# Gated linear attention on one core: decays, keys and states one head at a time, output gates between the values, a norm's factors spread ahead of the heads

## The chip, the core and the metric

The kernel runs on one core of one Trainium2 chip. TensorE (PE) multiplies, VectorE (DVE) and ScalarE (ACT) do element-wise work, GpSimd (POOL) a few powers, SyncE (SP) issues the loads. The metric is the device time of one execution in microseconds (us); of the kernel before, the median of three executions is 2082.17 us (2081.37 to 2084.97).

## What is computed

The program computes two transformer blocks of two layers each on 256 tokens of width 1024. The change lies in the last layer's mixer, gated linear attention with 4 heads, key width 128 and value width 256 per head, run over 256 context tokens and 256 latent tokens in both directions, in chunks of 64:

```python
q = z[..., :512] * 128 ** -0.5; k = z[..., 512:1024]; v = z[..., 1024:2048]; out_gate = z[..., 2048:]
g_d = log_sigmoid((h @ w_gate_down[d]) @ w_gate_up[d] + gate_bias[d]) / 16      # d: two directions
b = cumsum(g, within a chunk)
A = where(lower, (q * exp(b)) @ (k * exp(-b)).T, 0)
o = A @ v + (q * exp(b)) @ S
S = exp(b_last) * S + (k * exp(b_last - b)).T @ v                               # the state, chunk by chunk
o = rms_norm(o_forward + o_backward, g_norm) * silu(out_gate)
x = x + m[2] * rms_norm(o @ w_o, g_post_mix)                                    # then the channel MLP
```

## The kernel before, in words

Every weight is a granule of 128 x 1024 floats (512 KB). `gran` (line 483) takes the next granule in the order that `plan()` (line 34) writes out: `ahead` (line 460) keeps loads (SP), the high part `wh` (ScalarE, line 471) and the low part `wl` (VectorE, line 477) a few granules ahead, then the granule's matmuls are issued as three products each (high by high, high by low, low by high). What has to happen with a result (a copy out of PSUM) is deferred to the next granule or to `flush`.

Work off the weights is written as generators, added with `add` (line 508). `tick` (line 515) advances every generator that is alive by one step, in the order in which they were added; each granule ends with one such round, and the `steps(2)` of the mixer issue two more. The program is issued in exactly this order (a manual schedule), and each engine runs its own instructions in the order of issue. So an instruction that waits holds up everything issued after it on its engine.

In `layer2_gla` (line 1910), the order before is: queries of four heads (`gq`), two gate granules of head 0 (`gg` 0 and 1), the projection for the decays (`gdown`), then `decay()` is added; keys of four heads (`gk`); then the values of heads 0 to 3, two granules each (`gv`, 48 matmuls of 128 x 256 a granule); gates 2 to 7, 24 matmuls a granule; then the output projection (`gwo`).

- `decay()` (line 1956) makes the two directions' decays. Its first rounds fall among the keys: two matmuls a head into PSUM, Abs and Exp on ScalarE. Then, in one round for all heads, Ln (line 1975, with a load of its table); in the next two rounds the subtractions (line 1979, 128 x 1024, one a head), two heads a round; in two more the scans (lines 1985 and 1986, 128 x 512, two a head). Only after that `ldone` lets the heads begin.
- `direction(hd, d)` (line 2004) issues, a round each: (1) two small VectorE operations that begin `ke`; (2) five Exps on ScalarE; (3) three products on VectorE, `ke` first; (4) four transposes of `ke` and two score matmuls on TensorE; (5) the copy `gkn` on ScalarE (line 2039); (6) the first state's matmuls, which need `v`; (7) to (10) three more state matmuls, each with a state update on VectorE (line 2055).
- `outputs(hd)` (line 2061) follows when both directions are done: the mask on VectorE (line 2065), the output matmuls, copies and squares, the norm, transposes, the multiplication with the gate `og` (line 2097) and the split into `goT`, which `gwo` reads.
- `head(hd, delay)` (line 2108) adds the two directions, the second two rounds later, and the outputs. Head 0 is added ahead of the values of head 1, head 1 ahead of the values of head 3, heads 2 and 3 after all values, with delays 1, 1, 0 and 5.
- `bcast_cols(gmix, "G")` (line 1399) spreads the factors of the norm after the mixer over the partitions: eight transposes into two banks, each copied out by ScalarE. Before, it stands after the values (line 2151).

Of the kernel before, what the change touches and what calls it, by code (L numbers as in the profile page):

```python
# [33 lines left out]
def plan():  # L34

    g = []

    def ws(key, w, l, c0):
        g.append((key, w, l, "ws", 0, c0))

    def nat(key, w, l, r0, c0):
        g.append((key, w, l, "nat", r0, c0))

    def qkv(st, cb):
        for kp in range(4):
            nat(("qkv", st, cb, kp), "attn_w_qkv_2", 0, kp * 256, cb * 512)

    def awo(st):
        for hf in range(2):
            for kp in range(4):  # L50
                nat(("awo", st, hf, kp), "attn_w_o_2", 0, kp * 256, hf * 512)

    def mi(q, st):
        for i in range(8):
            ws(("mi", 0, q * 8 + i, st), "w_mlp_in_2", 0, (q * 8 + i) * 128)

    def mo(q, st):
        for hf in range(2):
            for kp in range(4):
                nat(("mo", 0, q, hf, kp, st), "w_mlp_out_2", 0, q * 1024 + kp * 256, hf * 512)  # L60


    for l in range(2):
        if l == 0:
            for kp in range(4):
                for p in range(3):
                    nat(("va", l, p, kp), "w_in", l, kp * 256, a_col(2, p, 0))
                nat(("vm", l, 0, kp), "w_in", l, kp * 256, C_V)
        else:
            for n in range(12):  # L70
                nat(("va", l, n // 4, n % 4), "w_in", l, n % 4 * 256, a_col(2, n // 4, 0))
        g.append((("gates", l), "w_in", l, "gates", 0, C_G))
        for qd in range(2):
            for which in range(2):
                for p in range(3):
                    for j in range(2):
                        ws(("at", l, qd, which, p, j), "w_in", l, a_col(which, p, qd * 4 + j * 2))
        for h in range(1 - l, 2):
            for kp in range(4):
                nat(("vm", l, h, kp), "w_in", l, kp * 256, C_V + h * 512)  # L80
        for h in range(4):
            for which in range(2):
                for d in range(2):
                    ws(("qk", l, h, which, d), "w_in", l, C_QK + which * 1024 + h * 256 + d * 128)
            for j in range(2 * h, 2 * h + 2):
                ws(("o", l, j), "w_in", l, C_O + j * 128)
            for kind, j in EXTRA[h]:
                if kind == "br":
                    ws(("br", l, j), "w_in", l, C_BR + j * 128)
                else:  # L90
                    g.append((("wb", l, j), "w_b", l, "wsb", 0, j * 256))
        for j in range(8):
            ws(("wa", l, j), "w_a", l, j * 128)
        for j in range(8):
            ws(("wo", l, j), "w_out", l, j * 128)
        if l == 0:
            for cb in (2, 0, 1):
                qkv(1, cb)
        else:
            mi(0, 1)  # L100
        for n, i in FF:
            if n == 1:
                ws(("w1", l, i), "w1", l, i * 128)
                ws(("w3", l, i), "w3", l, i * 128)
            else:
                g.append((("w2", l, i), "w2", l, "row", i * 128, 0))
        if l == 0:
            awo(1)
        else:
            mo(0, 1)  # L110
            mi(1, 1)
    for cb in (2, 0, 1):
        qkv(0, cb)
    mo(1, 1)
    awo(0)
    mi(2, 1)
    for q in range(3):
        mi(q, 0)
        mo(q, 0 if q < 2 else 2)
    mi(3, 2)  # L120
    for st in range(2):
        mo(3, st)
    for h in range(4):
        ws(("gq", h), "gla_w_in_2", 0, h * 128)
    for j in range(2):
        ws(("gg", j), "gla_w_in_2", 0, 2048 + j * 128)
    g.append((("gdown",), "gla_w_gate_down_2", 0, "gdown", 0, 0))
    for h in range(4):
        ws(("gk", h), "gla_w_in_2", 0, 512 + h * 128)
    for h in range(4):  # L130
        for hf in range(2):
            g.append((("gv", h, hf), "gla_w_in_2", 0, "wsb", hf * 512, 1024 + h * 256))
    for j in range(2, 8):
        ws(("gg", j), "gla_w_in_2", 0, 2048 + j * 128)
    for hf in range(2):
        for kp in range(4):
            nat(("gwo", hf, kp), "gla_w_o_2", 0, kp * 256, hf * 512)
    for n, i in LAST:
        if n == "mi":
            ws(("mi", 1, i), "w_mlp_in_2", 1, i * 128)  # L140
        else:
            g.append((("mo", 1, i), "w_mlp_out_2", 1, "row", i * 128, 0))
    n = len(g)
    for w in ("w_ada", "w_mod_2"):
        for l in range(2):
            for v in ADA_ORDER:
                for j in range(8):
                    g.append(((w, l, v, j), w, l, "colT", 0, v * 1024 + j * 128))
    return g, n
# [192 lines left out]
class Core:  # L342
# [28 lines left out]
    @property  # L371
    def late(self):

        return self.dve - self.pe


class Kernel:
# [1532 lines left out]
    def layer2_gla(self, x, xc):  # L1910
        nc = self.nc
        h = self.h1
# [3 lines left out]
        for hd in range(4):  # L1916
            ps = self.mmb()
            self.grans2(("gq", hd), self.mm_ws(ps[:, 0:256], hl),
                        lambda hd=hd, ps=ps: nc.scalar.activation(out=qT[:, hd], in_=ps[:, 0:256], func=AF.Copy, scale=128 ** -0.5))
        bank = [None]  # L1920

        def gates(j0, j1, gran):

            for j in range(j0, j1):
                if j % 2 == 0:
                    bank[0] = self.mmb()
                ps = bank[0]

                def post(j=j, ps=ps):
                    th = self.t2("gth", (128, 2, 256))  # L1930
                    nc.scalar.activation(out=th, in_=self.pair(ps), func=AF.Tanh, scale=0.5)
                    nc.vector.scalar_tensor_tensor(out=og.pair[j // 2], in0=th, scalar=1.0, in1=self.pair(ps), op0=ALU.add, op1=ALU.mult)
                gran(("gg", j), self.mm_ws(ps[:, (j % 2) * 256:(j % 2) * 256 + 256], hl), post if j % 2 else None)
        gates(0, 2, self.grans2)
        h[1] = self.wait(h[1])
# [15 lines left out]
        lg, ee, ldone = [None] * 4, [None] * 4, []  # L1951
# [4 lines left out]
        def decay():  # L1956
# [17 lines left out]
            for hd in range(4):  # L1974
                nc.scalar.activation(out=ee[hd], in_=ee[hd], func=AF.Ln, bias=1.0)
            yield
            for hd in range(4):
                f = lg[hd].rearrange("p a b -> p (a b)")
                nc.vector.tensor_tensor(out=f, in0=f, in1=ee[hd].rearrange("p a b -> p (a b)"), op=ALU.subtract)
                if hd % 2:  # L1980
                    yield

            for hd in range(4):
                B = ee[hd]
                nc.vector.tensor_tensor_scan(out=B[:, 0], data0=reset[:, 0], data1=lg[hd][:, 0], initial=0.0, op0=ALU.mult, op1=ALU.add)
                nc.vector.tensor_tensor_scan(out=B[:, 1, ::-1], data0=reset[:, 1, ::-1], data1=lg[hd][:, 1, ::-1], initial=0.0,
                                             op0=ALU.mult, op1=ALU.add)
                if hd % 2:
                    yield
            ldone.append(1)  # L1990
        self.add(decay())
        kT = [self.tv("gkT", (128, 2, 512)) for _ in range(2)]
        for hd in range(4):
            ps = self.mmb()
            self.gran(("gk", hd), self.mm_ws2(ps, h), lambda hd=hd, ps=ps: nc.scalar.activation(out=kT[hd // 2][:, hd % 2], in_=ps, func=AF.Copy))
            if hd:
                self.tick(False)
        v = [None] * 4
        ss = self.small([128, 2, 4], "gss", 1)
        i16 = 1.0 / 16  # L2000
        order = (0, 1, 2, 3), (3, 2, 1, 0)
        H = [dict(S=[None, None], qd=[None, None], at=None, done=0) for _ in range(4)]

        def direction(hd, d):
            k = kT[hd // 2][:, hd % 2]
            B = ee[hd][:, d]
            last, tot = (B[:, 63:256:64], B[:, 511:512]) if d == 0 else (B[:, 0:256:64], B[:, 256:257])
# [30 lines left out]
            kn = H[hd]["kn"][:, d]  # L2038
            nc.scalar.activation(out=kn.rearrange("p a b -> p (a b)"), in_=tr, func=AF.Copy)
            yield  # L2040
            st = self.aux()
            for b in range(2):
                nc.tensor.matmul(st[:, 0:256], kn[:, 2 + b], v[hd][:, 2 + b], start=b == 0, stop=b == 1)
# [17 lines left out]
        def outputs(hd):  # L2061
# [28 lines left out]
            for jj in range(2):  # L2090
                for b in range(2):
                    nc.tensor.transpose(tr[:, jj * 256 + b * 128:jj * 256 + b * 128 + 128], on[:, b, jj * 128:(jj + 1) * 128], self.ident)
            yield
            o32 = self.t2("go32", (128, 2, 256))
            for jj in range(2):
                nc.scalar.activation(out=o32[:, jj], in_=tr[:, jj * 256:(jj + 1) * 256], func=AF.Copy, scale=gn[:, jj:jj + 1])
# [8 lines left out]
        ot = [None] * 4  # L2105
# [7 lines left out]
        def values(hd):  # L2113
# [18 lines left out]
                return f  # L2132
            for hf in range(2):
                self.gran(("gv", hd, hf), mm(hf))
                steps(2)
        while self.adaq:
            self.ada_step()
        gmix = self.gain_cols(1, "g_post_mix_2", 2, 0)
        cols = self.scales(1, "g_pre_mlp_2", 3, 4, (0,))
        for hd in range(4):  # L2140
            if hd == 1:
                self.until(lambda: ldone)
                head(0, 1)
            if hd == 3:
                head(1, 1)
            values(hd)
        self.flush()
        head(2, 0)
        head(3, 5)
        oT = Lazy(lambda k: ot[k // 2][:, k % 2])  # L2150
        G = self.bcast_cols(gmix, "G")
        for j in range(2, 8):
            gates(j, j + 1, self.gran)
            steps(2)
        self.flush()
        y = [[None] * 2 for _ in range(2)]
        for hf, bank in enumerate((self.mmb, self.aux)):
# [98 lines left out]
```

## Time and profile before

| what | us |
|---|---|
| median of three executions | 2082.17 |
| lowest and highest | 2081.37, 2084.97 |
| the profiled execution's own time | 2092.44 |
| its span, first to last instruction | 2090.7 |
| mean granted clock of TensorE | 0.993 |

The profile is of one execution; its times run from the start of its span. A group is a kind of instruction on one engine, named by what it writes and reads (`trb<-ident,ke` are transposes of `ke` into a PSUM bank of that name). An arrow behind an idle time names the instruction whose end let the engine go on.

### The profile page before, as it was taken

The page shows a single profiled execution, that of the slowest core. Times are in us where ns is not written, and L with a number is a line of the kernel's source. Part 1 is how long each engine was busy: PE and PEld are TensorE (multiplying, and loading weights), DVE is VectorE, ACT ScalarE, POOL GpSimd, SP SyncE. Part 2 cuts the span into 40 slices and gives each one's busy share as a digit, 9 for nine tenths or more (in the row PEclk, how much of TensorE's full clock was granted, in tenths as well). Part 3 has the DMA queues.
Part 4 walks back from the last instruction along what each step waited for, and adds up shares of the span by engine and source line. Part 5 has one row for each costly group of instructions (what it writes and reads, how often), then busy time and mean ns, then how long its engine had stood idle before and what let it go on. Part 6 is the DMA issues. An engine that isn't in the chain of part 4 may idle for free.

```text
span 2090.7 us, 38245 instructions
## 1 busy us (share of the span) xinstructions
PE 2030.9 (97%) x15176; PEld 1888.9 (90%) x15176; DVE 1586.6 (76%) x2717; ACT 1149.3 (55%) x1968; POOL 45.1 (2%) x63
## 2 busy tenths in 40 slices
PE   7999999999999999998999999999999999999998
PEld 6999998899998989998999988899998989877997
DVE  7788988799978989988899776777563485466555
ACT  5756665655546656665744455556542464445444
POOL 0000000000000000000000000000000010000000
PEclk9999999999999999999999999999999999999999
DMA  9786566598876886555589755115553352214553
GB/s 340 281 320 213 192 235 221 187 315 305 304 254 228 284 274 233 187 202 186 167 290 358 274 196 176 61 56 176 191 183 101 115 181 75 77 65 155 188 191 132
DMA packets 120884, 426.88 MB, mean 204 GB/s; under 512 B 13664, under 2 KB 18528, under 8 KB 120704
## 3 DMA queue, kind: packets, MB, share of 16 engines
q1 hardware_dynamic: 120704, 424.43, 59.1%
q8 instruction: 119, 1.95, 0.4%
q14 instruction: 61, 0.50, 0.1%
HBM read 423.33 MB, written 1.05 MB: 203 GB/s over the span
## 4 chain that ended last, share of the span: by engine, by line
PE 87%; DVE 7%; ACT 4%; issue 1%; DMA 1%; POOL 0%; DVEq 0%; POOLq 0%; SPq 0%; ACTq 0%
PE mm L338 54%; PE aux L338 28%; PE trb L338 5%; DVE wl L338 1%; ACT wh L471 1%; DVE yg L338 1%; POOL rs L674 0%; ACT xh L1467 0%; DVE mtmp L338 0%; DMA raw<-in_w 0%; DVE xh L338 0%; DVE x L338 0%; DVE araw L338 0%; ACT ah L912 0%; DVE ee L338 0%
## 5 line engine op out<-in xcount | busy, mean ns | idle before, releaser
L338 DVE TENSOR_TENSOR wl<-raw,wh 128x1024 fp32r<-128x1024 f32 x591 | 718.7, 1221 | 153.1 <-PE aux L338 71.5
L471 ACT ACTIVATE wh<-raw 128x1024 fp32r<-128x1024 f32 x591 | 623.6, 1059 | 336.2 <-PE mm L338 117.7
L338 PE MATMUL mm<-uT,wh 128*128 128x256 f32 x3488 | 622.3, 282 | 0.0
L338 PEld LDWEIGHTS mm<-uT,wh 128*128 128x128 f32 x3488 | 531.7, 188 | 2.2 <-ACT va L814 0.3
L338 PE MATMUL mm<-uT,wl 128*128 128x256 f32 x1744 | 487.0, 279 | 0.0
L338 PE MATMUL mm<-hT,wh 128*128 128x256 f32 x1888 | 339.4, 283 | 4.8 <-ACT y L1772 2.1
L338 PEld LDWEIGHTS mm<-uT,wl 128*128 128x128 f32 x1744 | 329.6, 189 | 0.0
L338 PEld LDWEIGHTS mm<-hT,wh 128*128 128x128 f32 x1888 | 292.7, 190 | 11.5 <-ACT y L1772 2.3
L338 PE MATMUL mm<-hT,wl 128*128 128x256 f32 x944 | 265.8, 282 | 0.0
L338 DVE CUSTOM_DVE_ANT_0 araw<-araw,silu 128x1024 f32<-128x1024 f32 x192 | 233.2, 1220 | 8.4 <-DMA araw<-in_w 5.9
L338 PE MATMUL aux<-wh,hid 128*128 128x512 f32 x640 | 199.9, 394 | 0.0
L338 PEld LDWEIGHTS mm<-hT,wl 128*128 128x128 f32 x944 | 181.4, 192 | 0.0
L338 PEld LDWEIGHTS aux<-wh,hid 128*128 128x128 f32 x640 | 117.7, 188 | 23.6 <-DVE hid L338 0.2
L338 DVE TENSOR_TENSOR r<-r 128x256 f32<-128x256 f32 (+1 forms) x88 | 39.5, 448 | 117.4 <-ACT r L1905 117.3
L338 PE MATMUL aux<-mlg,wh 128*128 128x256 f32 x704 | 127.1, 283 | 0.0
L338 PE MATMUL aux<-wl,hid 128*128 128x512 f32 x320 | 124.8, 390 | 0.0
L338 PEld LDWEIGHTS aux<-mlg,wh 128*128 128x128 f32 x704 | 107.3, 188 | 0.0
L1905 ACT ACTIVATE r<-mm 128x256 f32<-128x256 f32 (+1 forms) x88 | 35.7, 406 | 125.1 <-PE mm L338 125.1
L338 PE MATMUL aux<-mlg,wl 128*128 128x256 f32 x352 | 98.8, 281 | 0.0
L674 POOL TENSOR_TENSOR rs<-ve,mhalf 128x1 f32<-128x1 f32 (+1 forms) x48 | 41.8, 871 | 2040.5 <-DVE ve L338 1853.0
L338 DVE CUSTOM_DVE_ANT_0 junk<-araw,silu 128x1024 bf16<-128x1024 f32 x64 | 77.9, 1218 | 0.0
L338 PE MATMUL mm<-wh,hT 128*128 128x256 f32 (+1 forms) x352 | 76.8, 316 | 0.6 <-DVE qs L338 0.6
(365 smaller groups left out, 3081.7 us busy)
## 6 DMA issues: line engine op xcount, KB each, us to landing
raw<-in_w SPq DMA_DIRECT2D x591, 512.0 KB, 3.9
araw<-in_w SPq DMA_DIRECT2D x192, 512.0 KB, 5.2
abias<-in_abias SPq DMA_DIRECT2D x32, 192.0 KB, 5.6
xc<-in_ctx SPq DMA_DIRECT2D x4, 512.0 KB, 6.1
x<-in_x SPq DMA_DIRECT2D x2, 512.0 KB, 4.2
gb<-in_ln SPq DMA_DIRECT2D x2, 512.0 KB, 5.4
out_x<-x SPq DMA_DIRECT2D x4, 256.0 KB, 2.0
mk<-in_mmask SPq DMA_DIRECT2D x1, 512.0 KB, 5.9
```

The costliest lines, as they stand in the source:

```text
L338: return f(*a, **k)
L471: nc.scalar.activation(out=wh, in_=self.raws[self.nhi], func=AF.Copy)
L674: nc.gpsimd.tensor_tensor(out=rs, in0=ve, in1=self.mhalf[:, 0:n], op=ALU.pow)
L1905: nc.scalar.activation(out=r[:, 0:n], in_=ps, func=AF.Relu)
```

## The change

Five things change. (a) In `plan()` and in the loop over the heads, the gates of heads 1, 2 and 3 follow the values of the same head instead of standing after all values. (b) `decay()` does the subtraction and both scans of one head in one round, for the four heads in four rounds, and appends each head to `ldone`; a direction waits for its own head only. Matmuls, Abs, Exp and Ln of the decays stay as they were. (c) Each head is added just ahead of its own values, with delays 0, 2, 0 and 0. (d) The factors of the norm are spread after the keys of head 2. (e) Two guards are new: a direction waits, ahead of its step 6, until its values have been issued (`vdone`), and the outputs until the gate has been issued (`gdone`).

```diff
-    for j in range(2, 8):
-        ws(("gg", j), "gla_w_in_2", 0, 2048 + j * 128)
+        for j in range(2 * h, 2 * h + 2) if h else ():
+            ws(("gg", j), "gla_w_in_2", 0, 2048 + j * 128)
...
+DELAY = (0, 2, 0, 0)
...
+            yield
+
             for hd in range(4):
                 f = lg[hd].rearrange("p a b -> p (a b)")
                 nc.vector.tensor_tensor(out=f, in0=f, in1=ee[hd].rearrange("p a b -> p (a b)"), op=ALU.subtract)
-                if hd % 2:
-                    yield
-
-            for hd in range(4):
                 B = ee[hd]
                 nc.vector.tensor_tensor_scan(out=B[:, 0], data0=reset[:, 0], data1=lg[hd][:, 0], initial=0.0, op0=ALU.mult, op1=ALU.add)
                 nc.vector.tensor_tensor_scan(out=B[:, 1, ::-1], data0=reset[:, 1, ::-1], data1=lg[hd][:, 1, ::-1], initial=0.0,
                                              op0=ALU.mult, op1=ALU.add)
-                if hd % 2:
-                    yield
-            ldone.append(1)
+                ldone.append(hd)
+                yield
         self.add(decay())
+        while self.adaq:
+            self.ada_step()
+        gmix = self.gain_cols(1, "g_post_mix_2", 2, 0)
+        cols = self.scales(1, "g_pre_mlp_2", 3, 4, (0,))
         kT = [self.tv("gkT", (128, 2, 512)) for _ in range(2)]
         for hd in range(4):
...
             if hd:
                 self.tick(False)
+            if hd == 2:
+                G = self.bcast_cols(gmix, "G")
...
         def direction(hd, d):
+            while hd not in ldone:
+                yield
...
+            while hd not in vdone:
+                yield
             st = self.aux()
...
+            while hd not in gdone:
+                yield
             o32 = self.t2("go32", (128, 2, 256))
...
-        while self.adaq:
-            self.ada_step()
-        gmix = self.gain_cols(1, "g_post_mix_2", 2, 0)
-        cols = self.scales(1, "g_pre_mlp_2", 3, 4, (0,))
+        oT = Lazy(lambda k: ot[k // 2][:, k % 2])
         for hd in range(4):
-            if hd == 1:
-                self.until(lambda: ldone)
-                head(0, 1)
-            if hd == 3:
-                head(1, 1)
+            head(hd, DELAY[hd])
             values(hd)
-        self.flush()
-        head(2, 0)
-        head(3, 5)
-        oT = Lazy(lambda k: ot[k // 2][:, k % 2])
-        G = self.bcast_cols(gmix, "G")
-        for j in range(2, 8):
-            gates(j, j + 1, self.gran)
-            steps(2)
+            self.flush()
+            if hd:
+                gates(2 * hd, 2 * hd + 1, self.gran)
+                steps(2)
+                gates(2 * hd + 1, 2 * hd + 2, self.gran)
+                steps(2)
         self.flush()
```

## Rows read from the trace of the kernel before

**Rows 1.** The page's first part: busy time and share of the span, each engine.
```profile
PE 2030.9 (97%) x15176; PEld 1888.9 (90%) x15176; DVE 1586.6 (76%) x2717; ACT 1149.3 (55%) x1968; POOL 45.1 (2%) x63
```
**Rows 2.** Waits of TensorE, 1738 to 1893.3: us in total, times, longest.
```profile
PE trb L338 <- DVE ke L338: 2.8, 1, 2.8
PE trb L338 <- ACT gkn L2039: 1.3, 1, 1.3
PE aux L338 <- DVE gS L338: 1.1, 3, 0.7
PE aux L338 <- ACT wh L471: 1.0, 1, 1.0
PE trb L338 <- ACT G L1407: 0.7, 1, 0.7
PE aux L338 <- DVE ATm L338: 0.6, 1, 0.6
PE aux L338 <- ACT gS L2047: 0.3, 1, 0.3
```
**Rows 3.** Chain that ended last, 1765 to 1782: start, length, what.
```profile
1769.28 5.58 DVE ee L338 x5
...
1776.12 1.28 ACT L2015
```
**Rows 4.** Granted clock (PEclk, behind the five engines) around that wait.
```profile
1778.00:1780.00 2.00, 0.99 (x5) 0.75 (x6) 1.74 (x5) 2.00 (x6) 0.00 (x0) 0.87 0.82 281
1780.00:1782.00 2.00, 2.00 (x11) 2.00 (x11) 0.43 (x2) 2.00 (x7) 0.00 (x0) 0.50 0.28 113
1782.00:1784.00 2.00, 2.00 (x15) 2.00 (x15) 2.00 (x4) 1.69 (x3) 0.00 (x0) 0.78 0.00 0
```
**Rows 5.** The same view, around the waits of the norm's factors.
```profile
1815.00:1820.00 5.00, 3.05 (x26) 2.57 (x25) 2.50 (x4) 3.52 (x9) 0.00 (x0) 1.00 0.16 48
```
**Rows 6.** VectorE in order of time, 1755 to 1790: start, length, instruction.
```profile
1760.15 4.63 DVE L338 TENSOR_TENSOR lg<-lg,ee 128x1024 f32<-128x1024 f32 x4 [2.71 <-ACT ee L1975]
1764.70 1.22 DVE L338 TENSOR_TENSOR wl<-raw,wh 128x1024 fp32r<-128x1024 f32 x1
1765.83 9.03 DVE L338 TENSOR_TENSOR_SCAN ee<-reset,lg 128x512 f32<-128x512 f32 x8
...
1775.95 0.41 DVE L338 TENSOR_TENSOR ke<-ee 128x256 f32<-128x256 f32 x1
...
1778.26 0.69 DVE L338 TENSOR_TENSOR ke<-ke,gkT 128x512 f32<-128x512 f32 x1 [0.75 <-ACT ke L2016]
1778.87 0.42 DVE L338 TENSOR_TENSOR gqk<-gqk,gqT 128x256 f32<-128x256 f32 x1
```
**Rows 7.** ScalarE in order of time, 1750 to 1767.
```profile
1757.76 1.28 ACT L1975 ACT_TABLE_LOAD   x1
1759.05 3.91 ACT L1975 ACTIVATE ee<-ee 128x1024 f32<-128x1024 f32 x4
...
1765.32 0.60 ACT L2131 ACTIVATE gv<-mm 128x512 f32<-128x512 f32 x1 [0.93 <-PE mm L338]
```
**Rows 8.** TensorE in order of time, 1910 to 1930: eight transposes that spread factors.
```profile
1926.32 1.03 PE L338 MATMUL trb<-ident,qgc 128*128 128x128 f32 x8
```
**Rows 9.** Chain, around 1832: transposes and scores of one direction.
```profile
1832.18 0.44 PE trb L338 x4
1832.62 0.45 PE aux L338 x4
```
**Rows 10.** Chain, from the end of a values granule to TensorE's next start.
```profile
1814.19 0.60 ACT gv L2131
...
1816.20 0.49 ACT gkn L2039
```
**Rows 11.** VectorE, 1850 to 1900: masking the scores.
```profile
1865.30 0.72 DVE L338 COPY_PREDICATED ATm<-tri,aux 128x512 f32<-128x512 int32 x1
```
**Rows 12.** VectorE, 1800 to 1850: second copy of an output.
```profile
1809.33 0.42 DVE L338 COPY gon<-aux 128x256 f32<-128x256 f32 x1 [0.54 <-ACT gsq L2082]
```

More of the change, by code (lines that the diff above doesn't have):

```diff
@@ L1919, in layer2_gla @@
                         lambda hd=hd, ps=ps: nc.scalar.activation(out=qT[:, hd], in_=ps[:, 0:256], func=AF.Copy, scale=128 ** -0.5))
-        bank = [None]
+        bank, gdone = [None], []
         def gates(j0, j1, gran):
@@ L1932, in post @@
                     nc.vector.scalar_tensor_tensor(out=og.pair[j // 2], in0=th, scalar=1.0, in1=self.pair(ps), op0=ALU.add, op1=ALU.mult)
+                    gdone.append(j // 2)
                 gran(("gg", j), self.mm_ws(ps[:, (j % 2) * 256:(j % 2) * 256 + 256], hl), post if j % 2 else None)
@@ L1997, in layer2_gla @@
                 self.tick(False)
-        v = [None] * 4
+            if hd == 2:
+                G = self.bcast_cols(gmix, "G")
+        v, vdone = [None] * 4, []
         ss = self.small([128, 2, 4], "gss", 1)
@@ L2134, in values @@
                 self.gran(("gv", hd, hf), mm(hf))
+                if hf:
+                    vdone.append(hd)
                 steps(2)
-        while self.adaq:
-            self.ada_step()
-        gmix = self.gain_cols(1, "g_post_mix_2", 2, 0)
-        cols = self.scales(1, "g_pre_mlp_2", 3, 4, (0,))
+        oT = Lazy(lambda k: ot[k // 2][:, k % 2])
         for hd in range(4):
-            if hd == 1:
-                self.until(lambda: ldone)
-                head(0, 1)
-            if hd == 3:
-                head(1, 1)
-            values(hd)
-        self.flush()
-        head(2, 0)
-        head(3, 5)
-        oT = Lazy(lambda k: ot[k // 2][:, k % 2])
-        G = self.bcast_cols(gmix, "G")
-        for j in range(2, 8):
-            gates(j, j + 1, self.gran)
-            steps(2)
+            head(hd, DELAY[hd])
+            values(hd)
+            self.flush()
[4 more added lines that the diff above has]
+                steps(2)
         self.flush()
```

## Prediction

> **What bounds the kernel now.** I read the page's busy times first, then TensorE's waits in the stretch that the change touches, then the chain of waits there, then each engine in order of time. TensorE is busy for 97% of the span [rows 1], so the reader should take it as the bound: a microsecond that it stands still is a microsecond of the result, and an engine beside it matters only where TensorE waits for it. From 1738 to 1893.3 TensorE waits 7.8 us in all [rows 2]. That is all there is to win, but for the clock. The largest wait, 2.8 us, is for `ke` of head 0. The chain there runs over the scans and a table load [rows 3]: VectorE is late with the decays, not TensorE with its work. After that wait the granted clock is 0.87, 0.50 and 0.78 over three stretches of 2 us [rows 4]; at the lower level (0.50, that is 1.2 of 2.4 GHz) these are 0.5 + 2.0 + 0.9 = 3.4 us, and half of it, 1.7 us, is lost. So head 0 costs 2.8 + 1.7 = 4.5 us before. The two waits around the norm's factors, 1.3 and 0.7 us [rows 2], left the clock at 1.00 [rows 5]. The other four groups of waits make 1.1 + 1.0 + 0.6 + 0.3 = 3.0 us [rows 2].
>
> **Head 0, the main term.** Number the rounds from the first after the first values granule. `decay()` has taken seven steps among the keys, so round 1 issues Ln, as before. Round 2 issues head 0's subtraction and scans, and then, in the same round, head 0's first direction begins `ke`. Round 3: head 1's decay, the Exps, and the second direction's start. Then the second values granule. Round 4: head 2's decay, and only behind it the products of the first direction. Round 5: head 3's decay, then the second direction's products on VectorE, and on TensorE the transposes of `ke`. Round 6: the second direction's transposes. Only then the values of head 1. Before, head 0 came one head's values later, so that two more granules covered the decays.
>
> VectorE's queue up to the first `ke` product is therefore: decay of head 0, start of `ke`, decay of head 1, start of `ke`, one `wl`, decay of head 2, product. A decay is one subtraction, 4.63 / 4 = 1.16 us, and two scans, 9.03 / 8 = 1.13 us each: 3.42 us. A start is 0.4 us, a `wl` 1.13 us from start to start, the product 0.69 us [rows 6]. The sum is 3 x 3.42 + 2 x 0.41 + 1.13 + 0.69 = 12.9 us. It begins when the first Ln is done, 1760.15 before [rows 6]. ScalarE has no pause between the table load and the Lns [rows 7], so the factors' eight transposes, now ahead of the last keys, push it back by their issue time, 0.8 us (a row of 1.03 us, of which the last overlaps the next matmul) [rows 8]: 1760.95. The product is ready at 1773.8. TensorE ends the second values granule when its copy begins, at 1765.3 [rows 7], or 1766.1 with the transposes: a wait of 7.7 us. Its transposes and scores take 0.44 + 0.45 = 0.9 us [rows 9]. The second direction's product comes after two more products (0.34 us each from start to start), head 3's decay and 0.69 us: 1778.6 [rows 6]. From 1766.1 to 1778.6 TensorE has 0.9 us of work and loses 11.6 us; with 1.7 us for the clock, as before, 13.3 us. Against 4.5 us that is **+8.8 us**. Looked at otherwise: `ke` comes 4.4 us earlier than the 1778.26 of before, but TensorE asks for it a whole head's values earlier. The Exps and the table load (1.28 us [rows 7]) lie beside head 1's and head 2's decays; without this cover they would cost some 3 us.
>
> **The factors.** Among the keys the transposes find both banks free, and the waits of 1.3 and 0.7 us go [rows 2]: **-2.0 us**. Their two copies on ScalarE lie in its idle time among the keys. The transposes themselves are moved, not added.
>
> **The later heads.** Each head now meets its values. The pattern is on record: where the second direction's Exps are issued just behind a values granule, ScalarE takes the last copy of the values, the Exps and then `gkn`, 1814.19 to 1816.7, 2.5 us [rows 10], and whatever on TensorE needs `gkn` waits.
> - Head 1 (delay 2): behind its second values granule come Exps, products, transposes: values copy 0.6, about half the Exps 0.7, product 0.69, or 2.0 us, less up to 1.3 us of head 0's state matmuls; 0.7 to 1.5 us, 1.1 taken.
> - Head 1's mask stands between its last state update and its outputs, with no granule between. The mask takes 0.72 us [rows 11] behind an update (longest wait 0.7): 0.6 [rows 2] to 1.4, 1.2 taken, since both now fall together.
> - Head 2: transposes, `gkn` and the first state fall in three rounds behind one granule. In ScalarE's queue head 1's two squares come first, and between them a copy on VectorE that waits 0.54 for the first square and takes 0.42 [rows 12]: some 1.5 us. So 2.5 + 1.5 - 0.9 = 3.1 us. A wait of 2.8 us dropped the clock, so I add 1.7 us; the ends are 1.2 us (no squares in the way, no clock) and 4.8.
> - Head 3: the same, with no squares and four more transposes as cover: 2.5 - 1.3 = 1.2 us.
> - The last outputs end one round later among the output projection's granules, with one granule less beside their norm: 0 to 1.6 us, 0.8 taken, next to the waits of 0.3 to 0.7 [rows 2].
>
> Together 1.1 + 1.2 + 3.1 + 1.2 + 0.8 = 7.4 us, and 1.7 of clock, against 3.0 that goes: **+6.1 us**.
>
> **What costs nothing.** The guards: `vdone` is set two rounds ahead of the first step that asks, `gdone` likewise; nobody waits. The loads: the same granules in another order, five ahead on SP; no wait of TensorE in this stretch is for a load [rows 2]. Without that cover a late granule would cost up to its landing time. The amount of work is the same on every engine.
>
> **Sum.** 8.8 - 2.0 + 6.1 = +12.9 us on the profiled execution's 2092.44, which is 10.3 us above the median of the runs. On the median, 2082.17 + 12.9 = 2095.1 us.
>
> **Rivals.**
> 1. *Only head 0 pays.* The heads no longer overlap in pairs, so the old 3.0 us go and no new waits come: 8.8 - 2.0 - 3.0 = +3.8 us, 2086 us. For it: buffers in PSUM are shared by fewer heads. Against: ScalarE's 2.5 us [rows 10] stand behind three heads now.
> 2. *Faster.* VectorE gets head 0's product out ahead of the other decays. Then `ke` needs 3.42 + 0.41 us, the table load, two Exps of some 0.4 and 0.69: 1767.6, a wait of 1.5 us and no drop of the clock. That is 1.5 - 4.5 = -3.0; with -2.0 for the factors and -3.0 for waits of heads that no longer meet, -8.0 us, 2074 us. The point that decides: head 0's waits and clock must stay under 4.5 + 2.0 = 6.5 us, if the later waits are as before. Against it is the order of the generators in a round: the decays are added first.
> 3. *The clock suffers from every wait.* Four further waits of about a microsecond each pay 1.7 us: +6.8, 2102 us. Against: the clock stayed at 1.00 over 1.3 and 0.7 us of waiting [rows 5]. The Trainium skill, TensorE: Matmul & The Clock Gate, section "A second HAM failure mode: psum-queue depth-cycling", says that short idle times between groups of matmuls, if frequent, make the clock swing. By that rule this rival would be the forecast; the row does not bear it out.
> 4. *It doesn't do what it says.* Ln still comes for all heads at once, and TensorE's idle time is only dealt out anew: within 4 us, about 2083 us.
>
> **How the numbers follow.** About 0.2%, or 4.2 us, can be told from no change. My forecast has 0.68, rival 1 0.14 (most of it over the bound), rival 2 0.08, rival 3 0.05, rival 4 0.05. Slower: 0.68 + 0.10 + 0.05 = 0.83; same: 0.04 + 0.05 = 0.09; faster: 0.08. The range goes from rival 1, 2086 us, to rival 3 at 2102 us, which also holds head 2's upper end and later waits half as long again (+1.7 and +3.7 would be 2100). What lies outside is rivals 2 and 4 and a little above.
>
> **What would show it.** In the profile after: TensorE waits for `ke` twice, some 7.7 and 3.9 us (with transposes at the lower clock the second is shorter), just behind head 0's values; the clock is at 0.50 around them; no wait for the factors' copies; a wait for `gkn` of about 3 us behind head 2's values. I am wrong if `ke` of head 0 waits under 4 us, if VectorE does head 0's products ahead of head 2's scans, or if the time falls.

## The result and the profile after

| | before | after |
|---|---|---|
| median of six executions each, us | 2082.43 (all: 2080.32 to 2097.15) | 2109.47 (five of them: 2100.59 to 2109.55) |
| ratio after to before, 95% interval | | 1.0101 [1.0073, 1.0128] |
| the profiled execution, us | 2092.44 | 2109.53 |
| first copy of the keys to the start of the last matmul of the output projection ("the stage" below), us | 1733.0 to 1892.9: 159.9 | 1733.3 to 1912.4: 179.1 |
| of it TensorE stands still, us | 7.9 | 20.2 |
| of it lost to the lower clock while busy, us | 1.7 | 5.6 |
| the rest: the same matmuls at full clock, us | 150.3 | 153.3 |

The kernel is slower, as forecast, by more than forecast: 15 to 27 us by the interval, against 12.9. (One of the six executions after, 2402 us, was disturbed, as were two of the kernel before in the experiments, 5918 and 6750 us: the median above counts it and would be 2109.40 without it, while ranges, ratios and the medians below leave all three out.) The two profiled executions are 17.1 us apart, and the stage holds it: both reach its start within 0.4 us, it is 19.2 us longer, and what follows it is 2.4 us shorter. So the stage is what the experiments are judged by. What follows it has two lengths: 195.3 to 195.4 us in after, its repetition, decays spread, head 0 earlier, gates undone and decays in pairs, 197.7 to 198.2 in the other eight executions (names as in the table of executions below), so some 2.5 us of a stage's gain can be given back behind it; the last section says by what. "Stands still" is the span of the stage less TensorE's busy time; "lost" is the busy time of each slice times one minus its granted clock.

The page's first part, to hold against [rows 1], shows that no instruction was added: every count is the same, and yet TensorE's busy time grew by 5.5 us.

```profile
PE 2036.4 (97%) x15176; PEld 1892.5 (90%) x15176; DVE 1586.5 (75%) x2717; ACT 1150.2 (55%) x1968; POOL 46.5 (2%) x63
```

TensorE's waits in the kernel after, 1738 to 1913: what it waited for, us in total, times, the longest.

```profile
PE trb L338 <- DVE ke L338: 11.8, 3, 7.7
PE aux L338 <- ACT gkn L2047: 4.3, 2, 3.0
PE trb L338 <- DVE gon L338: 1.3, 1, 1.3
PE aux L338 <- DVE ATm L338: 1.2, 1, 1.2
PE mm L338 <- DVE og L338: 0.9, 1, 0.9
PE mm L338 <- DVE goT L338: 0.4, 1, 0.4
PE aux L338 <- DVE gS L338: 0.4, 1, 0.4
```

Against [rows 2]: the waits for `G` (0.7) and for `gkn` ahead of a transpose (1.3) are gone, which is the factors' part of the change; `ke` went from 2.8 to 11.8 us (7.7 and 2.8 for head 0, 1.3 for head 1); `gkn` is new as a wait of the state (3.0 for head 2, 1.3 for head 3).

The chain that ended last, around head 0 (start, length, what). Read it by the names: `lg` and `ee` are decays, and the numbers of the heads are not in the tile names, so the order is read from the code: head 0, head 1, head 2, and only then the product `ke`.

```profile
1761.52 1.24 DVE lg L338
...
1765.16 0.34 DVE ke L338
1765.50 1.15 DVE lg L338
...
1769.38 1.14 DVE wl L338
1770.52 1.15 DVE lg L338
...
1771.69 2.34 DVE ee L338 x2
1774.03 0.58 DVE ke L338
...
1778.79 0.59 DVE ke L338
1779.38 0.04 issue
1779.43 1.11 PE trb L338 x4
```

VectorE has no gap from 1761.52 to 1774.6, and most of this is not for head 0: of the 12.5 us to the product's start, two decays of 1.15 + 2.34 us (heads 1 and 2) and a `wl` of 1.14, together 8.1 us, are not head 0's. TensorE waits behind it, and its clock falls. The view by stretches (us; busy time and count of TensorE, its weight loads, VectorE, ScalarE, GpSimd; granted clock; DMA), first around head 0, then around head 2's `gkn`:

```profile
1768.00:1770.00 2.00, 0.00 (x0) 0.00 (x0) 2.00 (x4) 2.00 (x5) 0.00 (x0) 0.72 0.00 0
1770.00:1772.00 2.00, 0.00 (x0) 0.00 (x0) 1.97 (x3) 1.38 (x5) 0.00 (x0) 0.50 0.21 41
...
1774.00:1776.00 2.00, 1.34 (x6) 1.34 (x7) 2.00 (x5) 0.19 (x1) 0.00 (x0) 0.50 0.00 0
1776.00:1778.00 2.00, 0.63 (x3) 0.33 (x2) 1.97 (x3) 1.36 (x2) 0.00 (x0) 0.50 0.00 0
1778.00:1780.00 2.00, 0.57 (x3) 0.57 (x4) 2.00 (x5) 0.00 (x0) 0.00 (x0) 0.50 0.00 0
1780.00:1782.00 2.00, 2.00 (x11) 2.00 (x10) 1.18 (x2) 0.60 (x1) 0.00 (x0) 0.50 0.00 0
1782.00:1784.00 2.00, 2.00 (x17) 2.00 (x16) 0.00 (x0) 0.00 (x0) 0.00 (x0) 0.86 0.78 254
```

```profile
1838.00:1840.00 2.00, 2.00 (x6) 1.53 (x7) 1.67 (x4) 0.78 (x2) 0.00 (x0) 0.50 0.03 8
1840.00:1842.00 2.00, 2.00 (x11) 2.00 (x10) 0.00 (x0) 0.95 (x2) 0.00 (x0) 0.50 0.59 166
1842.00:1844.00 2.00, 2.00 (x11) 2.00 (x10) 0.00 (x0) 0.00 (x0) 0.00 (x0) 0.50 0.24 96
```

The chain ahead of head 2's wait: ScalarE takes the values copy, head 1's two squares with a copy on VectorE between them, five Exps, and only then `gkn`.

```profile
1833.99 0.60 ACT gv L2143
1834.58 0.38 ACT gsq L2092 x2
...
1834.98 0.44 DVE gon L338
...
1835.44 0.47 ACT gsq L2092 x2
...
1837.33 0.49 ACT gkn L2047
```

What a low clock costs is the busy time in it. Around head 0 TensorE is at the lower level through most of the wait itself, where it costs nothing; the busy parts are 1.3 + 0.6 + 0.6 + 2.0 us at 0.50 and 2.0 at 0.86, and half or 0.14 of each makes 2.5 us lost. Around head 2 a wait of 3.0 us is followed by 6 us of full work at 0.50, and 3.1 us are lost: the drop outlasts the wait.

### The profile page after: what moved, and what is told of

It is laid out like the page before. It is cut to its first block, busy times and chain, and to the rows that moved or that the text cites. A ratio compares the mean times of both kernels' runs of the same rounds, so it can differ in the third digit from the quotient of the medians.

```text
span 2107.8 us, 38242 instructions
## 1 busy us (share of the span) xinstructions
PE 2036.4 (97%) x15176; PEld 1892.5 (90%) x15176; DVE 1586.5 (75%) x2717; ACT 1150.2 (55%) x1968; POOL 46.5 (2%) x63
## 4 chain that ended last, share of the span: by engine, by line
PE 86%; DVE 7%; ACT 4%; issue 1%; POOL 1%; DMA 0%; DVEq 0%; POOLq 0%; SPq 0%; ACTq 0%
PE mm L338 53%; PE aux L338 28%; PE trb L338 5%; DVE wl L338 1%; ACT wh L474 1%; POOL rs L677 1%; DVE yg L338 1%; ACT xh L1470 0%; DVE mtmp L338 0%; DVE ee L338 0%; DVE xh L338 0%; ACT u L906 0%; DMA raw<-in_w 0%; DVE x L338 0%; DVE araw L338 0%
```

## The experiments

The theory (A in the expectations): VectorE's queue is the cause, because the decays of later heads are issued ahead of head 0's first products; the later heads add a second, smaller term behind their values, and the clock a third. The other letters are its rivals: that head 0 comes too early whatever the order on VectorE, that the place of the later heads' steps beside the values is what costs, and that the gates between the values do. Every edit below is to the kernel after unless it says otherwise. "Stage", "still" and "lost" are those of the first table, from the profiled execution of each run; ratios are to the kernel before on the same chip.

**Before, unchanged.** How far do two executions of one kernel differ, and where?

> The kernel before, unchanged. The profiled execution of it was 2092.4 us, 10 us above its median of 2082.4, while the changed kernel's was at its own median. If the 10 us belong to executions and not to kernels, the ratio is 1.000 with an interval of some 0.003 to 0.006 either way, single executions lie near 2081 or near 2092, and a profile taken at 2081 shows where the 10 us are. If they were a matter of the first profile alone, all executions lie within 4 us.

Ratio 1.0004 [0.9988, 1.0021]; medians 2085.66 us (12 executions) and 2085.81 (34, from 2077 to 2094). They spread over these ranges and don't gather near 2081 and 2092, as was expected. The stage took 160.0 us, still 7.2, lost 1.7, as before, while the profiled execution took 2084.75 us, 7.7 us less than the profiled one of before: the difference lies ahead of the stage, which begins at 1725.2 instead of 1733.0. So the stage repeats within a microsecond where the total does not.

**After, unchanged.** The same for the kernel after.

> The changed kernel, unchanged, beside many runs of the kernel before. In the traces the stretch from the first copy of the keys to the last matmul of the output projection took 160.0 us before (twice) and 179.1 us after; what lies ahead of it varied by 10 us from one execution to the next, whatever the kernel. If the stretch is the whole effect, it is again 179 +- 1 us and the ratio is 1.0092 (19.1 of 2084 us), 1.008 to 1.011. If the first comparison's 27 us between medians were real, the ratio is 1.012 or more.

Ratio 1.0102 [1.0072, 1.0132]; stage 178.3 us, still 20.2 again, and the same seven groups of waits to the tenth. Only the clock differs: 4.8 us lost, 3.1 around head 0 instead of 2.5 and 1.7 around head 2 instead of 3.1. The slowdown is the kernel's; whether it is the stage's 1.0092 or the 1.012 of the first medians, this interval can't tell.

**The decays of heads 1 to 3 spread over the rounds.** One line gives each of them four rounds instead of one, so that head 0's products are issued ahead of head 1's scans.

```diff
                 ldone.append(hd)
-                yield
+                for _ in range(4):
+                    yield
```

> The changed kernel, with three idle rounds put between one head's decay and the next, so that VectorE reaches head 0's products ahead of the other heads' scans; head 0 begins as early as in the changed kernel. Theory A (TensorE's 10.5 us of waiting for ke, and the slow clock behind it, come from the decays of heads 1 to 3 in front of head 0's products on VectorE): the two waits fall to 2 and 1.5 us, the drop of the clock there goes or gets short, 7 to 10 us less than the changed kernel's 2109, about 2100. Theory B (head 0 is simply begun too early; the Exps, the table load and the products would make TensorE wait in any order): the waits stay at 7 us or more, within 3 us of 2109.

Ratio 1.0046 [1.0027, 1.0066], stage 170.0 us: 9.1 of the 19.2 are gone with one line that takes no work away. TensorE's two largest waits in this kernel's stage:

```profile
PE trb L338 <- DVE ke L338: 4.4, 3, 1.9
PE aux L338 <- ACT gkn L2048: 4.3, 2, 3.0
```

Head 0's waits fell from 7.7 and 2.8 to 1.2 and 1.9 us, but its drop of the clock, expected to go or get short, stayed at 2.6 us lost: two waits close together paid as much as the long one. `gkn` and the waits behind it did not move, to the tenth. So A holds for head 0, and head 0 did not come too early as such: with VectorE's queue in another order it waits less than a third as long. The later heads are a term of their own.

**Head 0 seven rounds later, order of the decays as in the change.** The other way to remove head 0's wait.

```diff
-DELAY = (0, 2, 0, 0)
+DELAY = (7, 2, 0, 0)
```

> The changed kernel with head 0 delayed by 7 rounds, so that both granules of head 1's values stand in front of its transposes, as before the change; the decays stay in the changed order. Theory A and theory B alike: no wait for ke of head 0 and no slow clock there, 12 to 14 us less for that, given back in part because heads 0 and 1 now meet (1 to 4 us): 2097 to 2101. Theory C (what the change costs lies with the later heads and their Exps behind the values): within 4 us of 2109.

Ratio 1.0046 [1.0026, 1.0066], stage 169.8 us. As much was gained, but the expectation of no wait for `ke` was a miss:

```profile
PE trb L338 <- DVE ke L338: 4.5, 2, 2.6
PE aux L338 <- ACT gkn L2047: 2.6, 2, 1.3
```

All four decays now stand ahead of head 0, as in the kernel before, and behind them come the table load of 1.28 us and the Exps on ScalarE before any product can start. That is before's own wait of 2.8 us [rows 2, 3] over again. A later start hides the decays but leaves the chain behind them. Head 2's `gkn` fell from 3.0 to 1.3 here, with head 0's steps later; which of them made room was not followed up. The clock cost 4.3 us in two drops. The first, 2.6 us, is behind the two waits for `ke`. The second, 1.7 us, has no long wait ahead of it: from 1776 to 1800 TensorE waits once, 0.57 us at 1791.84, and from 1797.7 to 1801.1 its granted clock is 0.50, with TensorE busy throughout.

```profile
1798.00:1800.00 2.00, 2.00 (x11) 2.00 (x11) 2.00 (x6) 0.12 (x1) 0.00 (x0) 0.50 0.27 53
1800.00:1802.00 2.00, 2.00 (x15) 2.00 (x14) 0.18 (x1) 1.41 (x5) 0.00 (x0) 0.73 0.55 209
```

**Only the later heads' delays.** Head 0 is left alone; each later head is put one round later or earlier, so that its Exps do not fall behind the values' copies.

```diff
-DELAY = (0, 2, 0, 0)
+DELAY = (0, 1, 1, 1)
```

> The changed kernel with delays 0, 1, 1, 1: heads 1 to 3 are shifted by one round, so that their Exps, transposes and gkn no longer fall in three rounds behind one granule. Theory A says that head 0 costs about 10.5 us of waiting and 2.6 us of clock, and that the later heads cost the rest: here the waits for gkn (3.0 and 1.3 us), for head 1's ke (1.3 us) and the second drop of the clock (3 us) go, 6 to 9 us less than 2109, about 2101; head 0's waits of 7.7 and 2.8 us stay. Rival (PSUM buffers, not ScalarE's queue, hold the later heads up): less than 3 us less.

Ratio 1.0028 [1.0010, 1.0046], stage 165.3 us: 13.8 us gone, where 6 to 9 were expected. All of its waits:

```profile
PE trb L338 <- DVE ke L338: 10.5, 2, 7.7
PE trb L338 <- DVE gon L338: 0.9, 1, 0.9
```

Head 0's waits are those of the change, and every other is gone but one: still 11.9 us instead of 20.2. With them went head 2's drop of the clock (lost 3.0 instead of 5.6) and 2.9 us of the rest (150.4 instead of 153.3): 8.3 + 2.6 + 2.9 = 13.8. The waits alone come out as expected; the clock and the rest came on top. Behind the stage 2.8 us are given back (198.2 us instead of 195.4). So the later heads' term is a matter of one round each, and even so it was worth more than the 9.1 us that the spread decays gave for head 0.

**Both.** The spread decays, and delays that leave each head clear of the values' copies.

```diff
-DELAY = (0, 2, 0, 0)
+DELAY = (3, 1, 1, 1)
...
                 ldone.append(hd)
-                yield
+                for _ in range(4):
+                    yield
```

> The changed kernel with both repairs together: three idle rounds between one head's decay and the next, and delays 3, 1, 1, 1. Theory A (waits behind VectorE's decays at head 0, and behind ScalarE's Exps and values copies at the later heads, with the drops of the clock behind them): no wait over 1.5 us, no drop of the clock, idle time of TensorE in the stretch 2 to 4 us, the stretch 153 to 156 us against 160 before: 4 to 7 us less than the kernel before, ratio 0.9965 to 0.998. If the gates between the values are bad in themselves (theory D: slower matmuls, buffers in PSUM), the stretch stays over 160 us.

Ratio 0.9983 [0.9970, 0.9996], stage 158.7 us: the change with two lines altered is faster than the kernel before, though its stage is some 3 us over what was expected. The chain shows what is late next:

```profile
1806.71 0.60 ACT gv L2144
1807.31 0.53 ACT goT L660
...
1807.86 0.69 DVE goT L338
...
1808.63 0.60 DVE ke L338
...
1809.37 1.09 PE trb L338 x4
```

Head 0's outputs are split into `goT` on ScalarE and VectorE, for an output projection that is tens of microseconds away, ahead of head 2's `ke`; and ScalarE's half stands behind a values copy. TensorE waits 2.7 us, and 1.5 us more are lost to the clock. It is the first fault in small, and the other way round: an item's last work stands ahead of a later item's first product.

**Both, head 0 one round earlier.** To the version with both:

```diff
-DELAY = (3, 1, 1, 1)
+DELAY = (2, 1, 1, 1)
```

> The two repairs again, with delays 2, 1, 1, 1 in place of 3, 1, 1, 1. In the run with 3 the one long wait (2.7 us for ke of head 2, with a drop of the clock behind it) came because head 0's split into goT was issued in the same round as head 2's products and stood ahead of them on VectorE behind the values copy. One round earlier the split stands ahead of the granule. Theory A: that wait and that drop go, 3 to 4 us off the stretch of 158.7 us: 154 to 156 us, ratio to the kernel before 0.996 to 0.9975. If the wait has another cause, the stretch stays at 158 to 160 us.

A miss: ratio 1.0016 [0.9999, 1.0034], stage 160.1 us. Head 2's wait and its drop are gone, but head 0's transposes now fall ahead of head 1's first values granule, and the chain runs through the table load, with TensorE standing still from 1760.23 to 1763.76:

```profile
1760.87 1.28 ACT L2024
...
1762.17 0.51 ACT ke L2024
...
1763.01 0.70 DVE ke L338
...
1763.76 1.12 PE trb L338 x4
```

Still 5.5 us in all, lost 2.7: one round earlier took the granule of values away that covered a load and three instructions.

**Both, with head 0's split three rounds later.** To the version with both, the edit is:

```diff
             yield
+            for _ in range(0 if hd else 3):
+                yield
             t = self.t4("goT", (128, 2, 2, 256), F32R)
             self.split(t[:, :, 0], t[:, :, 1], o32)
```

> The two repairs with delays 3, 1, 1, 1 (the stretch was 158.7 us), and three idle rounds ahead of head 0's split into goT, so that the split leaves the round of head 2's products. In the run with 2, 1, 1, 1 the wait for ke of head 2 (2.7 us) and its drop of the clock went, but head 0's transposes came one granule earlier and waited 3.5 us. Theory A: here both go; no wait over 1.5 us, no drop of the clock, idle time of TensorE 3 to 5 us, the stretch 153.5 to 156 us against 160 before, ratio to the kernel before 0.996 to 0.998 (the pace of the matmuls may move it by 2 us either way). If the split was not the cause, the wait stays and the stretch is 158 to 160 us.

As expected: stage 155.1 us, ratio 0.9981 [0.9966, 0.9996] (medians 2085.82 against 2087.96 us). All waits that are left:

```profile
PE aux L338 <- DVE gS L338: 1.8, 2, 1.3
PE aux L338 <- ACT gkn L2048: 1.5, 3, 0.8
PE trb L338 <- DVE gon L338: 0.9, 1, 0.9
```

Still 4.7 us, and the clock is at 1.00 through the whole stage. It is 4.9 us under before's stage, and it beats both kernels; the totals bear out 1 to 7 us of that.

**One part alone.** First the factors alone, put into the kernel before (the `ada_step` loop, `gmix` and `cols` go ahead of the keys with it).

```diff
+            if hd == 2:
+                G = self.bcast_cols(gmix, "G")
...
-        G = self.bcast_cols(gmix, "G")
```

> The kernel before with part (d) alone, the norm's factors spread after the keys of head 2. The two waits of 1.3 and 0.7 us go; the stretch is 158 us (160.0 before). Rival: ScalarE is still late with gkn behind the values of head 3, and something else waits in place of the transposes: 159.5 to 160.5 us.

Stage 158.3 us, 1.6 less than before's, both waits around the factors gone; one execution, 2079.6 us. Second, the order inside `decay()` alone in the kernel before, with head 0 still waiting for all four heads.

```diff
-                if hd % 2:
-                    yield
-
-            for hd in range(4):
...
-            ldone.append(1)
+                ldone.append(hd)
+                yield
...
-                self.until(lambda: ldone)
+                self.until(lambda: len(ldone) == 4)
```

> The kernel before with part (b) alone, subtraction and scans one head at a time in four rounds; the heads begin where they began before (head 0 waits for all four decays). VectorE does the same work in another order ahead of head 0's products, so the wait for ke stays at 2 to 3 us and the stretch at 160 +- 1 us: the order of the decays costs nothing by itself, only together with the early begin of head 0. If the new order were harmful by itself (short instructions in turn, waits between a scan and the next subtraction), the wait would grow by more than 1 us.

Stage 159.9 us, as before; one execution, 2091.06 us. The wait for `ke` was 3.35 us, a little over the 2 to 3 expected (2.8 and 2.1 in the two executions of before), and no other grew. So one head's subtraction and scans a round cost about a microsecond of waiting at most by themselves, and the stage none. They cost when a head starts between them.

**One part undone.** The gates of heads 1 to 3 after all values again (in `plan()` too), the rest of the change kept:

```diff
-            if hd:
-                gates(2 * hd, 2 * hd + 1, self.gran)
-                steps(2)
-                gates(2 * hd + 1, 2 * hd + 2, self.gran)
-                steps(2)
+        for j in range(2, 8):
+            gates(j, j + 1, self.gran)
+            steps(2)
```

> The changed kernel with part (a) alone undone: gates 2 to 7 again behind all values, the heads still begun ahead of their own values. Theory A (the cost is the early begin and the engines' queues, not the place of the gates): the waits of 7.7 and 2.8 us for ke of head 0 stay as they are, the waits for gkn behind the values of heads 2 and 3 stay in some form, the stretch is 175 to 183 us (179 with the change). Theory D (the gates between the values cost the time): the stretch falls under 170 us.

Stage 176.9 us, one execution, 2102.96 us: of the 19.2 us, 2.2 went. Head 0 is untouched, and other waits took the place of the later heads':

```profile
PE trb L338 <- DVE ke L338: 11.8, 3, 7.7
PE aux L338 <- DVE gS L338: 3.9, 3, 1.9
```

The last of these, 1.9 us for `gS` with no other wait in the 12 us ahead of it, has the dearest drop of the clock in any of these stages behind it: 3.4 us lost.

So the gates between the values are not the cause. Then two heads a round in `decay()` again, as before the change, and all heads let go together:

```diff
+                if hd % 2:
+                    yield
+            for hd in range(4):
...
-                ldone.append(hd)
-                yield
+                if hd % 2:
+                    yield
+            ldone.extend(range(4))
```

> The changed kernel with part (b) alone undone: subtractions and scans two heads a round, all heads let go together at the end. Head 0 then cannot begin before round 6, its transposes come one granule later (behind the first granule of head 1's values), and VectorE still has all four decays ahead of them. Theory A: the wait for ke of head 0 is 5 to 8 us in place of 10.5, the stretch 3 to 6 us shorter than 179. If the decays one at a time were a help in the changed kernel, undoing them would make the stretch longer than 179 us.

Stage 174.4 us, one execution, 2096.23 us: 4.7 us less than after's, as expected.

```profile
PE aux L338 <- ACT gkn L2051: 7.2, 3, 4.7
PE trb L338 <- DVE ke L338: 6.6, 1, 6.6
```

With all four decays ahead, head 0's two directions come together, and TensorE waits once, 6.6 us, rather than twice, 10.5 us; a `gkn` wait of 4.7 us is new. So the early release of head 0, as the change makes it, gains nothing over letting all heads go together.

The profiled executions side by side (us; "rest" is the stage less still and lost):

| kernel | stage | still | lost | rest |
|---|---|---|---|---|
| before; again | 159.9; 160.0 | 7.9; 7.2 | 1.7; 1.7 | 150.3; 151.1 |
| after; again | 179.1; 178.3 | 20.2; 20.2 | 5.6; 4.8 | 153.3; 153.3 |
| decays spread | 170.0 | 12.9 | 4.3 | 152.8 |
| head 0 late | 169.8 | 11.6 | 4.3 | 153.9 |
| later heads' delays | 165.3 | 11.9 | 3.0 | 150.4 |
| both | 158.7 | 7.0 | 1.5 | 150.3 |
| both, head 0 earlier | 160.1 | 5.5 | 2.7 | 152.0 |
| both, split later | 155.1 | 4.7 | 0 | 150.4 |
| factors alone | 158.3 | 5.3 | 1.7 | 151.3 |
| decays' order alone | 159.9 | 8.4 | 1.6 | 149.9 |
| gates undone | 176.9 | 18.4 | 6.3 | 152.2 |
| decays in pairs | 174.4 | 18.4 | 3.5 | 152.6 |

## Why the prediction was right in direction and too small

The direction and the mechanism held. The time did not: 2109.5 us against 2095.1, with 2102 as the upper end of the range. Three steps failed: the busy time, taken as unchanged, the later heads' term, taken too small, and the transfer to the median. Point by point, by its own steps:

- *Head 0's queue.* It gave the product ready at 1773.8 and a wait of 7.7 us from 1766.1. VectorE had it ready at 1774.61, 0.8 us later, but TensorE also came 0.9 us later, at 1766.97, and waited 7.70 us: that the wait agrees to the tenth is luck, its cause is not. The second wait was put at 3.9 and was 2.8, because the transposes and scores in between ran at half the clock, 1.97 us instead of 0.9: the two waits and the work between them are 12.5 us, as forecast. With the clock head 0 cost 13.0 us against 13.3. (The remark that `ke` comes 4.4 us earlier sets the end of the new product against the start of the old one; the sum does not use it.)
- *The factors.* Minus 2.0 us forecast; both waits gone, and alone the part gave 1.6 us of the stage.
- *The later heads' waits.* Forecast and measured: head 1's `ke` 1.1 and 1.27, its mask 1.2 and 1.21, head 2's `gkn` 3.1 and 3.03, head 3's 1.2 and 1.26. The queue given for head 2 is the one in the chain above; at head 1 the last to end ahead of the product was a state update of head 0 on VectorE (1798.66), 0.25 us behind the Exps that the prediction took, so that size is in part luck. The last outputs were put at 0.8 and took 1.7 us (`gon` 1.32, `goT` 0.39); not foreseen were 0.86 us for `og` at the first granule of the output projection and 0.35 for `gS`. Together that is 9.7 us against 7.4. Time stood still rose by 12.3 us against 11.2 (19.0 forecast, less 7.8).
- *The clock: a term that was mis-sized.* The prediction took "1.7 us for the clock, as before" at head 0 and 1.7 at head 2, so +1.7 over before. Measured were 2.5 and 3.1, and +3.9. At head 0 the excess only makes up for the shorter second wait; at head 2 it is an error. It assumed that every drop costs what the one of before cost, and the drops in these stages cost 1.4 to 3.4 us. In the repetition head 2's cost 1.7, so this term alone varies by 1.4 us between two executions. Waits and clock of the later heads together: 12.8 us against 9.1.
- *"The amount of work is the same on every engine": the other failed step.* It let the busy time stand at before's. The same matmuls, with idle time and clock taken off, took 153.3 us instead of 150.3. The table has it at 149.9 to 151.3 in seven executions, the two of before among them, and at 152.0 to 153.9 in the other seven, so it comes with some orders of the heads and not with others. Sorted by what the matmuls read (each counted to the start of the next, at full clock), 1.5 of the 3.0 us are in the state products (`gv,gkn`: 17.2 us before, 18.8 after, the same in each repetition), 1.0 in the values' granules (45.4 and 46.4) and 0.6 in the first granules of the output projection. In before's repetition the values took 46.1 us, so that part fits the two paces of the last section; what makes the state products longer was not shown.
- *The transfer to the median.* The sum was made against an execution 10.3 us above its median and added to the median, as if such an offset were shared. After's profiled execution was at its own median, so most of the 14.4 us between forecast and measured median is this step. The profiled executions are 17.1 us apart and the medians 27.0; the interval, 15 to 27, and the repetition's, 15 to 27, hold the stage's 18 to 19 us in their lower half. Whether the medians really are further apart than the stages, and by what, was not shown.

So of the miss of 6.3 us in the stage (19.2 against 12.9) 3.0 are the busy time, 2.3 the later heads' waits and 1.4 the clock at head 2; head 0 came out 0.3 lower. The range's upper end, 2102 us, allowed for four more drops of the clock, or for later waits half as long again and a longer one at head 2, but for nothing in the busy time and no offset between sets of executions.

The rivals. "Only head 0 pays" fell: the later heads pay more than half, as the delays alone show. "Faster" fell on its own point: head 0 cost 7.7 + 2.8 + 2.5 us, over the 6.5 that decides. Its mechanism was sound, though: where an edit put head 0's product ahead of the other decays, the kernel became faster than before once the later heads were also moved. "Every wait drops the clock" was not borne out: the four waits of 1.2 to 1.3 us in the kernel after stand at a granted clock of 1.00, and in the version with the split later six waits of up to 1.3 us left it at 1.00 throughout. But a short wait is no safeguard: with head 0 late the clock fell 5 us behind a single wait of 0.57 us, and with the gates undone behind one of 1.9. The time it would give, 2102 us, was nearer than the forecast, but for another reason. The Trainium skill, TensorE: Matmul & The Clock Gate, section "A second HAM failure mode: psum-queue depth-cycling", describes idle times between groups of matmuls that are short and frequent enough to make the clock swing. No run here shows frequent ones at work: the four waits of the kernel after did not do it, the two drops just named followed single waits, and what comes nearest is the spread decays' two waits of 1.2 and 1.9 us close together, which lost 2.6 us. "It does not do what it says" fell: the waits are where the code puts them, and the kernel is slower.

## What to carry to other kernels

When work is regrouped by item, write down each in-order engine's queue as the new issue order makes it, and look for the later items' early steps ahead of the first item's late ones: letting an item start first does not let it finish first. Put a step that is only needed at the end (a split for a later projection) behind the next item's first product, and judge each start by which stretch of other work still covers its chain: here one round more or less for each of the three later heads was worth 13.8 us of the stage. Judge such a change by its stage in the trace, not by totals that differ by 10 us for other reasons.

## What the runs showed of the hardware that was not expected

**Two paces at one clock.** Executions of the kernel before differ by up to 17 us (2077 to 2094 in 34), and in the two that were profiled the difference lies ahead of the stage. The same products run at one of two paces, both at a granted clock of 1.00, and keep it over long stretches. TensorE's groups from 1060 to 1210, count, busy time and mean ns, in the profiled execution of before and then in its repetition:

```profile
L338 PE MATMUL mm<-uT,wh 128*128 128x256 f32 x579 | 103.2, 281 | 0.0
```

```profile
L338 PE MATMUL mm<-uT,wh 128*128 128x256 f32 x595 | 102.1, 276 | 0.0
```

Fewer matmuls in the same 150 us, each 5 ns longer, and no idle time in either. In slices of 25 us from 1075 to 1175 the first has 214 or 215 matmuls on record and the second 223 in each of the four, 4% more. Some records can be missing from a trace, but not in so even a manner. It also explains the two lengths behind the stage: in the 80 us that begin 20 us behind it, both executions of before have 524 and 523 matmuls on record and both of after 531, with no idle time. What sets the pace, and what changes it, was not found; in the repetition it changes near 1495 us with no wait of TensorE between 1450 and 1520. With such differences between executions an interval of a few tenths of a per cent needs a dozen of them here.

**A drop of the clock outlasts its wait and has no fixed price.** Single waits of 2.1 to 3.4 us ahead of head 0 or 2 lost 1.5 to 1.7 us and one of 3.5 lost 2.7; one of 3.0 lost 1.7 in one execution and 3.1 in another of the same kernel. Nor does the length of the wait give it: one of 4.7 us lost 1.4 and one of 6.6 lost 2.0 (decays in pairs), but one of 1.9 lost 3.4 (gates undone), and 1.7 were lost behind one of 0.57 (head 0 late). Two waits of 1.2 and 1.9 us lost 2.6, about as much as one of 7.7 with one of 2.8 (2.5 to 3.1): in the long wait most of the low clock falls on an engine that has nothing to do.
